# A larger padding tile on the right side of SBUF: 96 bytes become 1504

## The chip, the core and the metric

The kernel runs on one core of one Trainium2 chip. The metric is the device time of one launch in microseconds; lower is better. Times of a kernel are given as the median of several runs, and one further execution, taken by the hardware profiler, gives the trace.

## What is computed

One decoder layer on 512 tokens of width 2048, in float32:

```
h = RMSNorm(x)
[qA|kA|vA|qB|kB|vB|gA|gB] = h @ W_in                 # 2048 x 8704
yA = sliding-window attention(qA,kA,vA) @ W_branch_a  # window 128, ALiBi, sinks
yB = stick-breaking attention(qB,kB,vB) @ W_branch_b
x = x + (sigmoid(gA)*yA + sigmoid(gB)*yB) @ W_out
x = x + SwiGLU(RMSNorm(x))                            # 2048 -> 2*5632 -> 2048
out = RMSNorm_final(x)
```

## The kernel before

**Matmuls in three parts.** Each float32 operand is split into a high part (rounded to the float32r type) and a low remainder. A product is three float32r matmuls: high by high, high by low, low by high. ScalarE writes the high part of a weight chunk (`whi`, line 153) and VectorE the low part (`wlo`, line 154), from a raw chunk that SyncE's queue has loaded. A matmul has a stationary operand of 128 columns (512 bytes in each partition), loaded into the array ahead of it, and a moving operand that streams through, mostly 512 columns (2048 bytes in each partition).

**Stages, in order.**
1. Input projection. `features` (lines 340 to 342) has weights stationary and the activations `fh`, `fl` moving, 512 columns wide: 896 chunks of three matmuls, and 96 matmuls of the same shape at lines 451 to 453. `tokens` (lines 356 to 358) has `fh`, `fl` stationary and weights moving, 256 columns wide: 960 matmuls. The two attentions run in small pieces between these.
2. Branch projections: `features` again, the same lines 340 to 342, now with `yh`, `yl` moving: 768 matmuls.
3. Output projection: `rows` (lines 856 to 858), `mh`, `ml` stationary, weights moving: 768 matmuls.
4. Feed-forward: `product` (lines 256 to 258), forms `fx` stationary, weights moving. It uses a Strassen-like scheme with seven products named p1 to p7. The gate-and-up part takes 11 groups x 7 names x 4 chunks x 12 matmuls = 3696; a chunk j reads the form pairs 2j and 2j+1, six matmuls each. The down projection takes 1848, again twelve to a chunk, six for each of two pairs. At its start the forms come back from DRAM through GpSimd's queue (`load_forms`, line 1022).

**Where the tiles lie.** SBUF is filled from both ends. From the left: pool `cp` (constants), pool `wp` (raw, whi, wlo: three buffers of 4096 bytes each) and pool `tp` (47 slots of 2048 bytes: `yh`, `yl`, attention tiles, and much else). From the right: pool `pad` with one tile, then `ep` (32 slots of 2048 bytes: `fh`, `fl`, and later `mh`, `ml`), then `ca` (attention constants, 10240 bytes). After the output projection `ep` and `ca` are closed and pool `fp` takes their place below `pad` (21 form slots of 2048 bytes, and eight raw chunks).

The built program gives these addresses (bytes within a partition): `wp` starts at 18944 (whi at 31232, wlo at 43520) and `tp` at 55808, all of them 512 modulo 2048; `tp` ends at 152064. On the right, `pad` lies at 229248, the first slot of `ep` at 227200 and the lowest tile of `ca` at 153472; the slots of `ep` and `fp` are at 1920 modulo 2048. Between the two sides 1408 bytes are free.

**Forms on both sides.** In the gate-and-up part, the form pairs 0 to 4 lie in `tp`, the pairs 5 to 7 in `fp` (`form_slot`, line 866):

```
if p >= 5:
    return fp.tile([P, T], F32R, tag="fx", name=uid("fx"), bufs=21)
return slot("fx", F32R)
```

So of a name's four chunks, j = 0 and j = 1 read left-hand forms only, j = 2 one left and one right, j = 3 right-hand forms only. In the down projection, of every two forms one is in `fp` and one in `tp` (`load_forms`).

**Order of work.** Each engine follows the order of the program; the tile framework puts in the waits between a tile's writer, its readers and the next writer of the same buffer. The weights are filled two chunks ahead (`Weights.fill`), and the buffers of a chunk come free when its matmuls have run. The padding tile is read by nothing; GpSimd clears it at the start (line 114).

Of the kernel before, what the change touches and what calls it, by code (L numbers as in the profile page):

```python
# [9 lines left out]
F32 = mybir.dt.float32  # L10
# [6 lines left out]
P = 128  # L17
# [28 lines left out]
def kernel(  # L46
# [15 lines left out]
    nc = tc.nc  # L62
# [6 lines left out]
    tp = ctx.enter_context(tc.tile_pool(name="tp", bufs=47))  # L69
    early = ctx.enter_context(ExitStack())  # L70
    pad = ctx.enter_context(tc.tile_pool(name="pad", bufs=1, side="right"))
    unused = pad.tile([P, 24], F32, tag="pad", name="pad")
    ep = early.enter_context(tc.tile_pool(name="ep", bufs=32, side="right"))
    ca = early.enter_context(tc.tile_pool(name="ca", bufs=1, side="right"))
    ps = ctx.enter_context(tc.tile_pool(name="ps", bufs=4, space=bass.MemoryType.PSUM))
# [21 lines left out]
    def const(s, w, dt=F32):  # L97
        return cp.tile([P, w], dt, tag=s, name=s)
# [12 lines left out]

    ident = const("ident", P)
    make_identity(nc, ident)
    nc.gpsimd.memset(unused, 0.0)
    ones = const("ones", P)
    nc.vector.memset(ones, 1.0)

# [776 lines left out]
    for n in range(4):  # L894
        tag = ("mm", "at")[n % 2]
# [225 lines left out]
```

## Time and profile before

| | us |
|---|---|
| median of 3 runs | 2548.81 (2547.82 to 2552.52) |
| the profiled execution | 2547.38 |
| its span, first to last instruction | 2545.4 |
| TensorE busy in the span | 2502.8 |
| VectorE busy | 1980.7 |
| ScalarE busy | 1377.4 |
| GpSimd busy | 251.4 |

Busy time is how long an engine had an instruction running; overlapping matmuls are counted once. The mean duration of one matmul in the profile is longer than the distance between the starts of two neighbours, because a matmul is still draining when the next has begun. The distance of starts is what a stream of matmuls costs.

### The profile page before, as it was taken

How to read it: one execution, taken by the hardware profiler on the slowest of the kernel's cores; microseconds unless marked ns; L12 is line 12 of the kernel's file. 1: busy time of each engine (PE TensorE's matmuls, PEld its weight loads, DVE VectorE, ACT ScalarE, POOL GpSimd, SP SyncE). 2: the span in 40 equal slices, each digit the busy share in tenths (PEclk: the TensorE clock that was granted, in tenths of full speed). 3: DMA queues.
4: the chain of work that ended last, by engine and by line, in shares of the span. 5: the costliest groups of instructions: out<-in, count | busy, mean ns of one | idle time of the engine just before them, and what ended most of it. 6: DMA issues, size and time to landing. Idle time of an engine off the chain costs nothing.

```text
span 2545.4 us, 33168 instructions
## 1 busy us (share of the span) xinstructions
PE 2502.8 (98%) x11529; PEld 2065.6 (81%) x11529; DVE 1980.7 (78%) x3457; ACT 1377.4 (54%) x2626; POOL 251.4 (10%) x482
## 2 busy tenths in 40 slices
PE   9999999999999999999999999999999999999997
PEld 8888878888887788888788888888888877888886
DVE  5688888888769644375788788888888877888888
ACT  6567777667657533265554555544555544333335
POOL 0000001111101000000010011100111024302100
PEclk9999999999999999999999999999999999999999
DMA  5232333333323644344456655566555689958652
GB/s 174 91 100 92 100 108 100 96 96 104 109 89 97 201 147 149 128 162 133 148 168 193 181 180 180 171 186 183 182 173 182 188 259 324 351 159 272 183 184 88
DMA packets 256295, 407.99 MB, mean 160 GB/s; under 512 B 16480, under 2 KB 103552, under 8 KB 256128
## 3 DMA queue, kind: packets, MB, share of 16 engines
q1 hardware_dynamic: 202096, 304.13, 38.5%
q0 software_dynamic: 46912, 89.15, 11.3%
q10 hardware_dynamic: 7120, 12.61, 1.3%
q8 instruction: 90, 1.47, 0.2%
q14 instruction: 77, 0.63, 0.1%
HBM read 344.48 MB, written 61.34 MB: 159 GB/s over the span
## 4 chain that ended last, share of the span: by engine, by line
PE 63%; issue 2%; ACT 1%; POOL 0%; DVE 0%; DMA 0%; ACTq 0%; POOLq 0%; DVEq 0%
PE mm L256 9%; PE mm L258 9%; PE mm L257 9%; PE at L256 7%; PE at L258 7%; PE at L257 7%; PE mm L341 3%; PE mm L342 3%; PE mm L340 3%; PE mm L856 1%; PE mm L857 1%; PE mm L858 1%; PE at L856 1%; PE at L858 1%; PE at L857 1%
## 5 line engine op out<-in xcount | busy, mean ns | idle before, releaser
L153 ACT CAST whi<-wx 128x1024 fp32r<-128x1024 f32 x264 | 277.2, 1050 | 333.5 <-PE at L258 150.5
L257 PE MATMUL mm<-wlo,fx 128*128 128x512 f32 x1056 | 417.3, 395 | 0.5 <-DVE wlo L154 0.5
L258 PE MATMUL mm<-whi,fx 128*128 128x512 f32 x1056 | 415.5, 393 | 0.0
L154 DVE TENSOR_TENSOR wlo<-wx,whi 128x1024 fp32r<-128x1024 f32 x264 | 322.6, 1223 | 112.4 <-ACT whi L153 110.5
L154 DVE TENSOR_TENSOR wlo<-raw,whi 128x1024 fp32r<-128x1024 f32 (+1 forms) x201 | 244.1, 1215 | 185.9 <-ACT whi L153 184.5
L256 PE MATMUL mm<-whi,fx 128*128 128x512 f32 x1056 | 375.7, 396 | 10.6 <-DMA fx<-f1p 5.5
L153 ACT CAST whi<-wz 128x1024 fp32r<-128x1024 f32 x198 | 207.8, 1050 | 283.0 <-PE mm L258 144.4
L342 PE MATMUL mm<-fh,wlo 128*128 128x512 f32 x896 | 354.9, 396 | 1.5 <-DVE wlo L154 1.5
L340 PE MATMUL mm<-fh,whi 128*128 128x512 f32 x896 | 354.8, 396 | 0.0
L341 PE MATMUL mm<-fl,whi 128*128 128x512 f32 x896 | 354.5, 396 | 0.0
L153 ACT CAST whi<-raw 128x1024 fp32r<-128x1024 f32 (+1 forms) x201 | 209.7, 1044 | 220.0 <-PE mm L341 131.2
L258 PE MATMUL at<-whi,fx 128*128 128x512 f32 x792 | 311.3, 393 | 0.0
L257 PE MATMUL at<-wlo,fx 128*128 128x512 f32 x792 | 310.8, 392 | 0.0
L593 ACT COPY turned<-z 32x128 f32<-32x128 f32 (+3 forms) x888 | 242.5, 273 | 106.0 <-DVE z L753 58.0
L154 DVE TENSOR_TENSOR wlo<-wz,whi 128x1024 fp32r<-128x1024 f32 x198 | 240.2, 1221 | 53.8 <-ACT whi L153 53.6
L256 PE MATMUL at<-whi,fx 128*128 128x512 f32 x792 | 279.8, 394 | 0.7 <-ACT whi L153 0.7
L256 PEld LDWEIGHTS mm<-whi,fx 128*128 128x128 f32 x1056 | 199.1, 189 | 53.9 <-DMA fx<-f1p 5.7
L257 PEld LDWEIGHTS mm<-wlo,fx 128*128 128x128 f32 x1056 | 199.5, 189 | 45.2 <-DVE wlo L154 1.7
L258 PEld LDWEIGHTS mm<-whi,fx 128*128 128x128 f32 x1056 | 199.5, 189 | 43.1
L342 PEld LDWEIGHTS mm<-fh,wlo 128*128 128x128 f32 x896 | 169.3, 189 | 42.2 <-DVE wlo L154 2.8
L341 PEld LDWEIGHTS mm<-fl,whi 128*128 128x128 f32 x896 | 169.5, 189 | 37.5
L340 PEld LDWEIGHTS mm<-fh,whi 128*128 128x128 f32 x896 | 169.2, 189 | 36.5
(254 smaller groups left out, 4177.8 us busy)
## 6 DMA issues: line engine op xcount, KB each, us to landing
raw<-in_w_in_dram SPq DMA_DIRECT2D x135, 512.0 KB, 3.6
raw<-in_w_ffn_in_dram SPq DMA_DIRECT2D x88, 512.0 KB, 3.7
wz<-in_w_ffn_in_dram SPq DMA_DIRECT2D x88, 512.0 KB, 4.4
wx<-in_w_ffn_in_dram SPq DMA_DIRECT2D x44, 512.0 KB, 4.4
raw<-in_w_ffn_down_dram SPq DMA_DIRECT2D x44, 512.0 KB, 4.2
wz<-in_w_ffn_down_dram SPq DMA_DIRECT2D x44, 512.0 KB, 5.0
raw<-in_w_out_dram SPq DMA_DIRECT2D x32, 512.0 KB, 3.6
wx<-in_w_ffn_down_dram SPq DMA_DIRECT2D x22, 512.0 KB, 5.5
```

The costliest lines, as they stand in the source:

```text
L153: nc.scalar.copy(hi[:, :n], raw[:, :n])
L154: nc.vector.tensor_tensor(out=lo[:, :n], in0=raw[:, :n], in1=f(hi[:, :n]), op=ALU.subtract)
L256: mm(banks[t], lhsT=hi, rhs=wh[:, kk, :], start=one, stop=False, skip_group_check=True)
L257: mm(banks[t], lhsT=hi, rhs=wl[:, kk, :], start=False, stop=False, skip_group_check=True)
L258: mm(banks[t], lhsT=lo, rhs=wh[:, kk, :], start=False, stop=end, skip_group_check=True)
L340: mm(b, lhsT=wh[:, kk, c], rhs=hi[k], start=(k == 0), stop=False)
L341: mm(b, lhsT=wh[:, kk, c], rhs=lo[k], start=False, stop=False)
L342: mm(b, lhsT=wl[:, kk, c], rhs=hi[k], start=False, stop=(k == nk - 1))
L593: copy(t4[c * Q : (c + 1) * Q, :, r], z4[r * Q : (r + 1) * Q, :, c])
L856: mm(banks[t], lhsT=hi[k][:, c], rhs=wh[:, kk, :], start=(k == 0), stop=False)
L857: mm(banks[t], lhsT=hi[k][:, c], rhs=wl[:, kk, :], start=False, stop=False)
L858: mm(banks[t], lhsT=lo[k][:, c], rhs=wh[:, kk, :], start=False, stop=(k == nk - 1))
```

## The change

The padding tile grows from 24 to 376 float32 columns, 96 to 1504 bytes in each partition. Everything to the right of the free gap, that is all slots of `ep`, `ca` and `fp`, moves down by 1408 bytes. No buffer is added or taken, and no other instruction changes, save that GpSimd clears 8 columns of the padding tile in place of all 24.

```diff
-    unused = pad.tile([P, 24], F32, tag="pad", name="pad")
+    unused = pad.tile([P, 376], F32, tag="pad", name="pad")
...
-    nc.gpsimd.memset(unused, 0.0)
+    nc.gpsimd.memset(unused[:, :8], 0.0)
```

## Rows read from the trace of the kernel before

**Rows 1.** The page: span and busy time by engine, granted TensorE clock in 40 slices.
```profile
span 2545.4 us, 33168 instructions
...
PE 2502.8 (98%) x11529; PEld 2065.6 (81%) x11529; DVE 1980.7 (78%) x3457; ACT 1377.4 (54%) x2626; POOL 251.4 (10%) x482
...
PEclk9999999999999999999999999999999999999999
```
**Rows 2.** Waits of TensorE, longest first: us in total, times, longest.
```profile
PE mm L256 <- DMA fx<-f1p: 5.5, 1, 5.5
PE mm L256 <- ACT whi L153: 5.1, 1, 5.1
PE at L417 <- DMA grow<-in_norm_ffn_g_dram: 4.3, 1, 4.3
```
**Rows 3.** Matmul groups by shape: count, busy us, mean ns of one, idle before.
```profile
L342 PE MATMUL mm<-fh,wlo 128*128 128x512 f32 x896 | 354.9, 396 | 1.5 <-DVE wlo L154 1.5
...
L342 PE MATMUL mm<-yh,wlo 128*128 128x512 f32 x256 | 99.6, 389 | 0.0
...
L356 PE MATMUL mm<-whi,fh 128*128 128x256 f32 x320 | 90.0, 282 | 0.0
...
L615 PE MATMUL at<-kah,q 128*128 128x256 f32 x64 | 16.1, 281 | 0.0
```
**Rows 4.** Three stretches with one kind of matmul each: us, TensorE busy and count, clock.
```profile
62.60:84.60 22.00, 22.00 (x97) 17.83 (x96) 6.85 (x9) 5.41 (x7) 0.00 (x0) 1.00 0.31 95
870.00:1036.00 166.00, 166.00 (x735) 137.47 (x734) 76.40 (x117) 60.22 (x77) 0.00 (x0) 1.00 0.46 149
1040.00:1212.00 172.00, 172.00 (x742) 139.46 (x741) 96.82 (x260) 86.61 (x198) 6.64 (x12) 1.00 0.43 138
```
**Rows 5.** TensorE in order of time, one name of the gate-and-up part.
```profile
1610.14 0.62 PE L256 MATMUL mm<-whi,fx 128*128 128x512 f32 x2
...
1612.87 0.62 PE L256 MATMUL mm<-whi,fx 128*128 128x512 f32 x2
...
1615.59 0.62 PE L256 MATMUL mm<-whi,fx 128*128 128x512 f32 x2
...
1618.35 0.63 PE L256 MATMUL mm<-whi,fx 128*128 128x512 f32 x2
```
**Rows 6.** The same view, a chunk j = 3 that nothing interrupts.
```profile
1642.23 0.64 PE L256 MATMUL at<-whi,fx 128*128 128x512 f32 x2
...
1644.09 0.40 PE L258 MATMUL at<-whi,fx 128*128 128x512 f32 x1
1644.33 0.40 PE L256 MATMUL at<-whi,fx 128*128 128x512 f32 x1
1644.57 0.39 PE L257 MATMUL at<-wlo,fx 128*128 128x512 f32 x1
...
1645.03 0.39 PE L256 MATMUL mm<-whi,fx 128*128 128x512 f32 x1
```
**Rows 7.** The same view, four attention matmuls among the input projection.
```profile
164.49 0.39 PE L658 MATMUL at<-ph,vv 128*128 128x512 f32 x1
...
165.43 0.39 PE L340 MATMUL mm<-fh,whi 128*128 128x512 f32 x1
```
**Rows 8.** The chain of waits at the start of the down projection.
```profile
2046.63 0.53 POOL f19p L990
...
2097.45 0.54 POOL x L1008
2098.00 5.72 DMA fx<-f1p
```
**Rows 9.** Stretches of gate-and-up and down: columns as in rows 4 (PE, PEld, DVE).
```profile
1500.00:1800.00 300.00, 300.00 (x1341) 245.72 (x1340) 251.03 (x286) 155.44 (x209) 25.86 (x49) 1.00 0.60 180
...
2300.00:2530.00 230.00, 230.00 (x999) 187.67 (x998) 197.20 (x215) 95.29 (x112) 24.73 (x46) 1.00 0.56 176
```
**Rows 10.** GpSimd in order of time, the clearing of the padding tile.
```profile
0.95 0.12 POOL L114 MEMSET pad<- 128x24 f32 x1
```
**Rows 11.** Instructions on the tiles `yh`: durations ns min/median/max, first and last start us.
```profile
L340 PE MATMUL mm<-yh,whi x256: 387/389/399, 863.9 to 1037.3; 128*128 128x512 f32 x128
```

## The prediction

> **What bounds the kernel now.** I read the page first: TensorE is busy for 2502.8 of 2545.4 us, VectorE for 78% and ScalarE for 54%, and the granted clock stands at 9 tenths or more of its higher level, 2.4 GHz, in every slice [rows 1]. Then I read what TensorE waited for: the three longest waits are 5.5, 5.1 and 4.3 us, once each [rows 2]. All its idle time is 2545.4 - 2502.8 = 42.6 us. So the kernel is a nearly unbroken stream of matmuls, and the only quantity that can move it much is the distance between the starts of two of them. The question for a change of addresses is whether this distance depends on where the operands lie.
>
> The trace answers it, because this kernel runs the same lines with operands on either side. I took stretches that hold one kind of 512-column matmul and divided the time by the count (one or two of the count still run from before the stretch, so I take off two) [rows 4]:
> - `features` with `fh`, `fl` moving, on the right: 22.00 / 95 = 231.6 ns.
> - `features` with `yh`, `yl` moving, on the left, the same three lines: 166.00 / 733 = 226.5 ns.
> - `rows` with `mh`, `ml` stationary, on the right: 172.00 / 740 = 232.4 ns.
>
> All three at a granted clock of 1.00, with no idle TensorE. The mean durations of single matmuls say the same: 396 ns with `fh`, 389 ns with `yh` on line 342 [rows 3]. These are different stages, though, so I looked for both sides within one stage. In the gate-and-up part, chunks j = 0 and j = 1 have their forms on the left, j = 2 half and half, j = 3 on the right. At 1610.14 us a name begins: its chunks of twelve take 2.73, 2.72 and 2.76 us [rows 5]; the fourth holds transposes, so for j = 3 I take an undisturbed one, 1642.23 to 1645.03, 2.80 us [rows 6]. That is 227, 227, 230 and 233 ns for a matmul, with the same neighbours on VectorE and ScalarE within 35 us. The weights lie on the left throughout. So a matmul whose two operands both lie on the left, at the same offset modulo 2048 in steps of 512, costs 227 ns, and one with an operand on each side costs 5 to 6 ns more, whichever operand it is.
>
> **The change, part by part.** The right side moves down by 1408 bytes: 1920 - 1408 = 512, the offset of the left side. If the extra 5 to 6 ns hang on the offset, all right-hand matmuls come to the left-hand spacing. The terms:
>
> 1. *Input projection, `fh` and `fl` moving.* 3 x 896 + 96 = 2784 matmuls. Per matmul, at least 231.6 - 226.5 = 5.1 ns [rows 4], at most 396 - 389 = 7 ns [rows 3]. I take 5.7, between them, near the difference that the longer stretch of `rows` shows (232.4 - 226.5 = 5.9): 15.9 us, bounds 14.2 and 19.5.
> 2. *Output projection, `mh` and `ml` stationary.* 768 matmuls at 232.4 - 226.5 = 5.9 ns, or 5.4 if they only come to the 227 of the left-hand chunks [rows 4, 5]: I take 5.6, 4.3 us, bounds 4.1 and 4.5.
> 3. *Feed-forward, right-hand forms.* In gate-and-up 3 of 8 pairs, 3696 x 3/8 = 1386; in down one of two, 924; together 2310. Per matmul (2.80 - 2.72) / 12 = 6.7 ns by the undisturbed chunks; by the mixed chunk (2.76 - 2.72) / 6 = 6.7 ns too, the starts being read to 0.01 us, so each is good to about 1 ns [rows 5, 6]. I take 6: 13.9 us, bounds 11.5 (5 ns) and 15.4.
> 4. *256-column matmuls of `tokens`, `fh` and `fl` stationary, 960.* The nearest all-left rows of that width are the attention scores: 281 ns against 282 [rows 3]. I take nothing. Bounds: the difference of the wide ones, 5.7 x 960 = 5.5 us gained, and, since 281 against 282 leaves 1 ns either way, 1 us lost.
> 5. *The clearing.* 0.12 us on GpSimd at 0.95 us after the start [rows 10], off TensorE's path; less of it changes nothing that I can see.
> 6. *The order and the waits.* No tile gains or loses a buffer. `pad`, `ep`, `ca` and `fp` move together, so each slot of `fp` covers the same slots of `ep` and `ca` as before, and waits for the same readers. The 1408 bytes are just those that were free. VectorE's and ScalarE's pieces are the same; where an address changes their speed, they have room: VectorE is busy 251.03 of 300 us in gate-and-up and 197.20 of 230 in down [rows 9], 84 and 86%, which a stream of matmuls 1.5% denser makes 85 to 87%.
>
> Against this stands what the stream gives back. Where TensorE waits for a chain that other engines set, it comes to the wait earlier by what it saved while the chain ran. The longest such chain is GpSimd's queue from 2046.63 to 2098.00, which issues the loads of the forms, ending in the wait for `f1p` [rows 8]: 51 us, some 220 matmuls, half of them on the right, 6 ns each: 0.7 us. The others are shorter; I take 1.2 us for all.
>
> Sum: 15.9 + 4.3 + 13.9 - 1.2 = 32.9 us. The profiled execution took 2547.38, the median of the runs is 1.43 above it; 2548.81 - 32.9 = 2515.9. I say 2516, which is 1.3% less.
>
> By the bounds: at most 19.5 + 4.5 + 15.4 + 5.5 = 44.9, that is 2504; at least 14.2 + 4.1 + 11.5 - 1 - 3 (more given back) = 25.8, that is 2523.
>
> **A rule that speaks against it.** The rows show a distance of starts that goes with the side on which an operand lies: 226.5 and 231.6 ns on the same three lines [rows 4]. The Trainium skill, page "SBUF — State Buffer", section "Who interferes with whom", gives TensorE two independent read ports, one for the moving operand and one for the weights, and says that "PE and ACT never wait on anyone". By that rule the place of an operand costs nothing and the change is worth nothing: 2548.8. The trace does not agree with it as far as it goes; that is rival A.
>
> **The rivals.**
>
> *A. Nothing moves.* The extra 5 to 6 ns belong to the right-hand part of the memory itself, or to something that goes with those tiles, and not to the offset; then 2548.8, within 5 us. For it: the trace holds right-hand tiles at one offset only, so side and offset can't be told apart in it. Also for it: four attention matmuls with both operands in `tp` go from 164.49 to 165.43, 235 ns each, though all of it lies on the left [rows 7]; so the common offset alone doesn't assure 227. Against it: these are a few dozen, between right-hand neighbours, while whole stages and thousands of forms on the left keep 227 from addresses 31232 up to 152064, so far apart that a border just above would be a strange chance.
>
> *B. The common offset is the bad one for right-hand tiles: slower.* Some right-hand matmuls are 0.24 us apart already, as from 1644.09 to 1644.33 and to 1644.57 [rows 6]. If a right-hand tile at 512 met the weights in this way every time, the 2784 + 768 + 2310 = 5862 matmuls would cost 240 - 232.4 = 7.6 ns more: 45 us, 2593. It turns to slower by over 5 us as soon as their mean spacing rises by 0.9 ns. Against it: left-hand tiles at that very offset, with the same weights, show none of it over 166 us [rows 4].
>
> *C. The stream speeds up, but the feed of the down projection doesn't follow.* There GpSimd's queue loads the forms as buffers come free and VectorE is at 86% [rows 9], and the wait of 5.5 us at the start shows that the loads can be late [rows 2, 8]. If each later part waited for its loads, the 924 x 6 = 5.5 us of the down projection would go, and with a like sum at its start some 10 us in all: 2526. Against it: from 2300 to 2530 TensorE has no idle time at all [rows 9].
>
> **How the numbers follow.** The forecast as it stands gets 0.84, A 0.07, B 0.04, C 0.05. A measurement of this kernel tells about 0.2%, 5 us, from no change. The forecast and C are faster: 0.89; A is the same: 0.07; B is slower: 0.04. The forecast's own range is 2504 to 2523; with C it reaches 2528, and the range 2504 to 2528 leaves out A, B and a little at each edge.
>
> **What would show it.** In the profile after: line 342 with `fh` at a mean of 389 ns in place of 396; lines 856 to 858 at 389 as well; all four chunks of a gate-and-up name at 2.72 us unless a transpose lies in them; the span shorter by about 16 us when the branch projections begin (863.9 us before [rows 11]), by 20 when the feed-forward does, and by 33 at the end; the branch projections unchanged. The steps fail if `fh` falls and `mh` or the right-hand forms don't (then moving and stationary operands differ), or if none falls (A). The prediction is wrong if the spacing stays at 232, or if it comes to 227 and new idle time before TensorE takes up more than 10 us.

## The result, and the profile after

The changed kernel takes 2522.24 us, median of 4 runs (2522.17 to 2522.51), against 2548.32 for the kernel before on the same chip: 0.9895 of its time, 95% interval 0.9878 to 0.9912. That is 26.1 us less; 32.9 were forecast, and the time lies within the range of 2504 to 2528, less than 1 us inside the forecast's own edge of 2523. The profiled execution took 2522.17 us, and every engine runs the same instructions in the same order as before, but for the clearing of the padding tile.

The page: TensorE's busy time has fallen by 30.5 us, its idle time (span less busy time) has risen from 42.6 to 47.9 [rows 1].

```profile
span 2520.2 us, 33168 instructions
...
PE 2472.3 (98%) x11529; PEld 2063.9 (82%) x11529; DVE 1979.0 (79%) x3457; ACT 1378.9 (55%) x2626; POOL 251.4 (10%) x482
```

Matmul groups by shape (columns as in [rows 3]). `fh` moving has come from 396 to 391 ns, `mh` stationary stands at 389, like the all-left `yh`, which hasn't moved. The 256-column `tokens` have gone up by 1 ns.

```profile
L342 PE MATMUL mm<-fh,wlo 128*128 128x512 f32 x896 | 350.8, 391 | 4.0 <-DVE wlo L154 3.9
...
L342 PE MATMUL mm<-yh,wlo 128*128 128x512 f32 x256 | 99.6, 389 | 0.0
...
L356 PE MATMUL mm<-whi,fh 128*128 128x256 f32 x320 | 90.3, 283 | 0.0
...
L857 PE MATMUL mm<-wlo,mh 128*128 128x512 f32 x128 | 49.8, 389 | 0.0
```

Two stretches of one kind each (columns as in [rows 4]), `yh` above, `mh` below. With two of each count taken off, both are 160.00 / 705 = 227.0 ns; `mh` was at 232.4. For `fh` and `fl` the mean of all distances of starts in the trace (those above 300 ns, where something interrupts, left out, as in all such means below) falls from 232.6 to 227.5.

```profile
870.00:1030.00 160.00, 160.00 (x707) 132.50 (x706) 73.86 (x114) 58.55 (x74) 0.00 (x0) 1.00 0.44 144
1040.00:1200.00 160.00, 160.00 (x707) 132.50 (x706) 93.59 (x252) 84.73 (x195) 6.63 (x12) 1.00 0.43 140
```

The starts of five chunks of twelve in the gate-and-up part, from TensorE in order of time: at 1592.21 a chunk j = 3 (all right), then j = 0 and 1 (all left) and j = 2 (mixed). All four take 2.72 us; they took 2.80, 2.73, 2.72 and 2.76 [rows 5, 6].

```profile
1592.21 0.61 PE L256 MATMUL at<-whi,fx 128*128 128x512 f32 x2
...
1594.93 0.61 PE L256 MATMUL mm<-whi,fx 128*128 128x512 f32 x2
...
1597.65 0.61 PE L256 MATMUL mm<-whi,fx 128*128 128x512 f32 x2
...
1600.37 0.61 PE L256 MATMUL mm<-whi,fx 128*128 128x512 f32 x2
...
1603.09 0.62 PE L256 MATMUL mm<-whi,fx 128*128 128x512 f32 x2
```

The same view, the four attention matmuls of [rows 7], whose tiles all lie on the left and have not moved: 0.91 us where they took 0.94.

```profile
162.16 0.39 PE L658 MATMUL at<-ph,vv 128*128 128x512 f32 x1
...
163.07 0.39 PE L340 MATMUL mm<-fh,whi 128*128 128x512 f32 x1
```

When the branch projections begin, only 7.0 us have been gained (856.9 for 863.9 [rows 11]), where 16 were forecast:

```profile
L340 PE MATMUL mm<-yh,whi x256: 389/389/389, 856.9 to 1030.3; 128*128 128x512 f32 x128
```

What TensorE waited for (us, times, longest). The first three are nearly as before [rows 2]; `wlo` at line 342 is new in this size, 3.9 in place of 1.5 [rows 3].

```profile
PE mm L256 <- DMA fx<-f1p: 5.8, 1, 5.8
PE mm L256 <- ACT whi L153: 5.1, 1, 5.1
PE at L417 <- DMA grow<-in_norm_ffn_g_dram: 4.3, 1, 4.3
PE at L658 <- ACT ph L598: 4.2, 1, 4.2
PE mm L342 <- DVE wlo L154: 3.9, 4, 1.8
```

One such wait costs twice. The end of the windowed attention, first in the kernel before, then in the changed one (columns as in [rows 4]): TensorE's idle time is 3.45 and then 4.37 us, and the granted clock, which falls from 2.4 to 1.2 GHz after the wait, stays low for longer, with a mean of 0.94 and then 0.89 of the higher level over these 30 us.

```profile
340.00:370.00 30.00, 26.55 (x109) 21.15 (x108) 21.73 (x51) 24.26 (x58) 0.00 (x0) 0.94 0.24 74
```

```profile
340.00:370.00 30.00, 25.63 (x101) 20.37 (x100) 22.58 (x49) 23.94 (x53) 0.00 (x0) 0.89 0.23 71
```

The start of the feed-forward shows the same in its clock alone, again before and then after. The wait there is 5.1 us in both kernels, but the granted clock of the 22 us around it is 0.84 and then 0.77. Why it stays low for longer there isn't shown.

```profile
1210.00:1232.00 22.00, 16.39 (x67) 12.75 (x66) 14.93 (x34) 13.80 (x29) 2.16 (x4) 0.84 0.67 239
```

```profile
1200.00:1222.00 22.00, 16.35 (x66) 12.74 (x66) 16.34 (x36) 14.10 (x30) 2.16 (x4) 0.77 0.67 239
```

### The profile page after: what moved, and what is told of

Read it like the earlier page. It is cut to its first block, busy times and chain, and to the rows that moved or that the text cites. A ratio compares the mean times of both kernels' runs of the same rounds, so it can differ in the third digit from the quotient of the medians.

```text
span 2520.2 us, 33168 instructions
## 1 busy us (share of the span) xinstructions
PE 2472.3 (98%) x11529; PEld 2063.9 (82%) x11529; DVE 1979.0 (79%) x3457; ACT 1378.9 (55%) x2626; POOL 251.4 (10%) x482
## 4 chain that ended last, share of the span: by engine, by line
PE 62%; issue 2%; DVE 1%; ACT 1%; POOL 0%; DMA 0%; ACTq 0%; POOLq 0%; DVEq 0%
PE mm L257 9%; PE mm L258 9%; PE mm L256 9%; PE at L256 7%; PE at L257 7%; PE at L258 7%; PE mm L340 3%; PE mm L341 3%; PE mm L342 3%; PE at L858 1%; PE mm L856 1%; PE mm L858 1%; PE at L856 1%; PE at L857 1%; PE mm L857 1%
## 5 line engine op out<-in xcount | busy, mean ns | idle before, releaser
L258 PE MATMUL at<-whi,fx 128*128 128x512 f32 x792 | 308.4, 389 | 0.0
L256 PE MATMUL at<-whi,fx 128*128 128x512 f32 x792 | 276.3, 389 | 0.7 <-ACT whi L153 0.7
```

The source lines that it names most:

```text
L256: mm(banks[t], lhsT=hi, rhs=wh[:, kk, :], start=one, stop=False, skip_group_check=True)
L258: mm(banks[t], lhsT=lo, rhs=wh[:, kk, :], start=False, stop=end, skip_group_check=True)
```

## The experiments

Three questions were open: do the stages add up as the steps say; which distance between the sides counts; and where some 7 us went. Each ratio is to runs of the kernel before that were made beside the run in question (medians from 2548.3 to 2549.1 us).

**One part of the change alone.** e1 puts the larger padding under the feed-forward's pool only, e2 under the input projection's pools only.

```diff
 # e1: padding tile of 24 columns, and before pool fp is opened:
+pad2 = ctx.enter_context(tc.tile_pool(name="pad2", bufs=1, side="right", ...))
+unused2 = pad2.tile([P, 352], F32, tag="pad2", name="pad2")
 # e2: the same tile in a pool that closes with ep and ca
+pad2 = early.enter_context(tc.tile_pool(name="pad2", bufs=1, side="right"))
```

> Only pool fp (feed-forward forms and chunks) moves to offset 512; ep and ca stay at 1920. Theory (each matmul pays for its own two operands): fh and mh keep 231 to 233 ns, all fx come to 227; 2310 x 6 = 13.9 us less, 1 to 2 given back: 2535 to 2537. Rival (the gain of the change comes from the input projection alone and the feed-forward is held by its feed): under 5 us less, 2543 or more.

> Only ep and ca (fh, fl, mh, ml, attention constants) move to 512; fp stays at 1920. Theory: fh and mh at 227 ns, right-hand fx at 233; 14 + 4 us less from the spacing, and most of what the change gave back to waits appears here, in the attention stage: 5 to 7 us; so 2535 to 2538. Rival (what was given back lies in the feed-forward): 2530 to 2531.

e1 took 2532.96 us, 0.9939 of before (0.9922 to 0.9956), 16.1 us less; e2 2537.18, 0.9954 (0.9939 to 0.9969), 11.9 less. Together 28.0, the whole change 26.1: the parts add up to within 2 us, and in the spans of the traces more closely (14.4 + 10.5 = 24.9 against 25.2). e1 lies 2 to 4 us below its forecast, e2 within its own. The windows show that each stage follows the place of its own right-hand tiles. e1, `mh` at the old place (160.00 / 688 = 232.6 ns), then the down projection (200.00 / 882 = 226.8):

```profile
1040.00:1200.00 160.00, 160.00 (x690) 129.73 (x689) 95.88 (x259) 85.83 (x197) 6.64 (x12) 1.00 0.44 142
2300.00:2500.00 200.00, 200.00 (x884) 165.68 (x883) 172.88 (x179) 81.42 (x89) 20.41 (x38) 1.00 0.59 187
```

e2, the same two stretches: the other way round (227.0, and 200.00 / 867 = 230.7).

```profile
1040.00:1200.00 160.00, 160.00 (x707) 132.55 (x706) 93.59 (x252) 84.72 (x195) 6.64 (x12) 1.00 0.44 140
2300.00:2500.00 200.00, 200.00 (x869) 163.20 (x869) 169.82 (x175) 79.87 (x88) 20.54 (x39) 1.00 0.59 187
```

e2 also begins the branch projections at 856.9 us, like the full change, so the 7.0 us belong to its first stage alone.

Within a stage, neighbours pay too. In the down projection of the kernel before, six matmuls with right-hand forms alternate with six with left-hand ones. The last left-hand one of six is 232.0 ns from the next start and the first 231.0, the four between them 226.8 to 227.3 (means of 149 each, the last part, which goes by threes, left out); in the changed kernel all six lie between 226.4 and 227.0.

**Which distance counts.** Four other paddings; e4 moves the left side too. The numbers at the right are the places modulo 2048.

```diff
-    unused = pad.tile([P, 376], F32, tag="pad", name="pad")
+    unused = pad.tile([P, 120], F32, tag="pad", name="pad")   # e3: right side at 1536
+    unused = pad.tile([P, 280], F32, tag="pad", name="pad")   # e4: right side at 896,
+    lunused = lpad.tile([P, 96], F32, tag="lpad", name="lpad")  #     and left at 896
+    unused = pad.tile([P, 312], F32, tag="pad", name="pad")   # e5: right side at 768
+    unused = pad.tile([P, 360], F32, tag="pad", name="pad")   # e11: right side at 576
```

> Padding of 480 bytes: right-hand tiles at 1536 modulo 2048, left at 512; equal modulo 512 and 1024, not modulo 2048. If equality modulo 2048 is what counts: spacing 231 to 233 ns with one operand on each side, 2545 to 2550. If modulo 512 is enough (the weights' slices lie at all four multiples of 512 and cost 227 in all): 227 ns, 2520 to 2524.

> A padding of 384 bytes on the left too, and 1120 on the right: all tiles at 896 modulo 2048, equal to each other, none at a multiple of 512. If the distance between the two operands counts: 227 ns everywhere, 2520 to 2524. If each operand's own place counts (a multiple of 512): every matmul at 231 to 233, the left-hand ones too: 2565 to 2580.

> Padding of 1248 bytes: right-hand tiles at 768 modulo 2048, 256 away from the left side modulo 512. Equality modulo 512 is what counts: 231 to 233 ns with one operand on each side, 2545 to 2550. Equality modulo 256 is enough: 227 ns, 2520 to 2524.

> Padding of 1440 bytes: right-hand tiles at 576 modulo 2048, 64 away from the left side modulo 256. If only a distance of 128 modulo 256 is bad: 227 ns, 2520 to 2524. If the distance has to be 0 modulo 256, or modulo 128: 231 to 240 ns with one operand on each side, 2545 or more.

| run | right less left, mod 2048 | us | of before (95%) |
|---|---|---|---|
| changed kernel | 0 | 2522.24 | 0.9895 (0.9878 to 0.9912) |
| e4, both at 896 | 0 | 2523.15 | 0.9898 (0.9883 to 0.9913) |
| e3 | 1024 | 2521.84 | 0.9895 (0.988 to 0.991) |
| e5 | 256 | 2522.58 | 0.9899 (0.9883 to 0.9916) |
| e11 | 64 | 2549.40 | 1.0006 (0.9997 to 1.0015) |
| before | 1408 = 5 x 256 + 128 | 2548.32 | |

The same stretch of `mh` in e3, e4, e5 and e11, one after the other:

```profile
1040.00:1200.00 160.00, 160.00 (x707) 132.49 (x706) 93.81 (x252) 84.73 (x195) 6.64 (x12) 1.00 0.43 140
```

```profile
1040.00:1200.00 160.00, 160.00 (x708) 132.48 (x707) 93.69 (x252) 84.75 (x195) 6.64 (x12) 1.00 0.43 140
```

```profile
1040.00:1200.00 160.00, 160.00 (x708) 132.48 (x707) 94.10 (x252) 85.48 (x196) 6.67 (x12) 1.00 0.44 143
```

```profile
1040.00:1200.00 160.00, 160.00 (x687) 128.93 (x686) 94.14 (x252) 85.93 (x196) 6.65 (x12) 1.00 0.43 140
```

About 707 matmuls in 160 us at a distance of 0, 256 or 1024, and 687 (160.00 / 685 = 233.6 ns) at 64. So it is the distance between the two sides that counts, not the place of either (e4), and equality modulo 2048 is more than is needed: the three distances tried that are multiples of 256 are all good. The fallen theories are the first one of e3 (modulo 2048), the second of e4 (each operand's own place), the first of e5 (modulo 512), and the first of e11 (that only 128 is bad).

These paddings move the right-hand tiles for every engine alike, so they don't say whose reads meet. A stretch in which VectorE, ScalarE and GpSimd do nothing does: the end of the output projection, first in the kernel before, then in the changed one (columns TensorE, weight loads, VectorE, ScalarE, GpSimd).

```profile
1202.30:1214.30 12.00, 12.00 (x53) 9.72 (x52) 0.00 (x0) 0.00 (x0) 0.00 (x0) 1.00 0.27 87
```

```profile
1191.25:1203.15 11.90, 11.90 (x54) 9.87 (x53) 0.00 (x0) 0.00 (x0) 0.00 (x0) 1.00 0.27 88
```

By the starts, 52 distances of `mh` from 1202.33 to 1214.42 have a mean of 232.5 ns, and 51 from 1191.43 to 1202.99 one of 226.7: the difference is whole without the other engines. Nor are transfers needed: 30 matmuls of `mh` in the kernel before and 33 in the changed one have no DMA packet and no other engine at work from 0.3 us before their start to the end of the next, and they lie at 232.4 and 226.7 ns. What is left of what the change moved is the two operands that TensorE reads itself.

**Where the rest went: load or chains.** e6 moves two of every 16 transposing copies from VectorE to ScalarE in both attentions, e8 does so in the kernel before; e7 and e12 set the windowed attention's pieces out more thinly or more densely (`pace` is how many of them come due at each step of the matmul stream).

```diff
-            split_turned(z, NT, ph, pl, 10)          # e6, e8
+            split_turned(z, NT, ph, pl, 12)
-            split_turned(z, NT - j, oh, ol, 8)
+            split_turned(z, NT - j, oh, ol, 10)
...
-        pace[0] = 0.36
+        pace[0] = 0.33                               # e7; 0.39 in e12
```

> The changed kernel with two more of every 16 transposing copies on ScalarE in both attentions (12 and 10 in place of 10 and 8). Theory (the 8 us given back are waits in the attention stages for a VectorE that is 88% busy there and that the denser stream outruns): the waits between 320 and 362 us and near 800 us fall from some 15 us to under 9, 2514 to 2518. Rival (the waits are the length of single chains, not VectorE's load): ScalarE's copies are slower, 273 ns against 217, the chains get longer, 2522 to 2526.

> The kernel before with the same shift of copies to ScalarE. Spacing stays at 232. Theory: before, the stream was slower and VectorE just kept up, so the shift is worth less here than in the changed kernel: 1 to 3 us, 2545 to 2547. Rival: it is worth as much or as little in both, because the waits have nothing to do with the density of the stream.

> The changed kernel with the windowed attention's pieces set out more thinly (pace 0.33 in place of 0.36). If VectorE's load in that stage is what TensorE waits for, pieces spread over more matmuls take 2 to 5 us of waits away: 2517 to 2520; the pieces moved behind the stage may bring them back later: 2522. Rival (single chains): no change, 2521 to 2523.

> The changed kernel with the windowed attention's pieces set out more densely (pace 0.39 in place of 0.36), since thinner cost 3 us. If the waits at the end of that stage come from pieces left over there: 2517 to 2520. If VectorE then falls behind earlier in the stage: 2523 to 2528.

e6 took 2529.59 us (0.9928 of before, 0.9913 to 0.9943), 7 more than the changed kernel and more than either theory said. e8 took 2557.17 (1.0034, 1.0021 to 1.0047), 9 more than before. So the loss is about the same with the old spacing as with the new, as the rival of e8 has it, and taking load from VectorE at ScalarE's cost doesn't shorten the waits: those for ScalarE's results at the end of the attention chains grew, in e6 from 4.2 to 7.4 us at line 658, and new ones at line 729:

```profile
PE at L658 <- ACT ph L598: 7.4, 5, 3.4
...
PE at L729 <- ACT a L743: 3.8, 3, 2.0
```

e7 took 2525.56 (0.9912, 0.9897 to 0.9926), 3 more, against both its theories; e12 2522.24 (0.9897, 0.9882 to 0.9912), no gain and between its two forecasts. These four also change the order in which pieces and matmuls are issued, so none of them singles out one cause. No version of the whole computation beats the changed kernel by more than the runs differ.

**Where the rest went: the chains taken away.** e9 (the changed kernel) and e10 (the kernel before) replace the 16 copies by one, which leaves the blocks in the wrong places. The two have the same order of instructions, save the clearing.

```diff
-        t = unblock(z, n, share)[:, : n * P]
+        t = slot("turned")[:, : n * P]
+        nc.scalar.copy(t, z[:, : n * P])
```

> The changed kernel with the 16 small copies after each block transpose in both attentions replaced by one ScalarE copy of the whole tile (the blocks then stay in the wrong places: part of the computation is left out). VectorE and ScalarE have far less to do there. Theory (the 8 us given back are waits for the attentions' chains, which a denser stream reaches earlier): the waits at 323, 334, 349 to 362, 778 and 798 us, 13.4 us together with the slow clock after them, go: 2503 to 2511, and 31 to 34 us less than the kernel before with the same cut. Rival (the shortfall lies in the spacing or elsewhere): 26 us less than that kernel, as now.

> The kernel before with the same cut (the blocks stay in the wrong places). Spacing of the right-hand matmuls stays at 231 to 233 ns; its attention waits at 355 and 805 us, 7.4 us, go: 2536 to 2543. Theory: 31 to 34 us above the changed kernel with the cut. Rival: 26 above.

e9 took 2498.31 us, e10 2531.41: 33.1 apart, as the theory said, though both fell by more than forecast (24 and 17 us less than with the copies; 11 to 19 and 5 to 12 were expected). The page, e9 and then e10:

```profile
span 2495.8 us, 31687 instructions
...
PE 2462.9 (99%) x11529; PEld 2061.5 (83%) x11529; DVE 1845.8 (74%) x2777; ACT 1214.1 (49%) x1926; POOL 250.1 (10%) x482
```

```profile
span 2530.0 us, 31687 instructions
...
PE 2497.2 (99%) x11529; PEld 2063.2 (82%) x11529; DVE 1848.3 (73%) x2777; ACT 1212.0 (48%) x1926; POOL 249.8 (10%) x482
```

TensorE's idle time is 32.9 and 32.8 us: where the attentions' chains don't hold it, both kernels wait alike, and the whole difference, 2497.2 - 2462.9 = 34.3 us, is spacing. Added up from start to start by kind of matmul in the two traces, it is 14.3 us for `fh` and `fl` with 512 columns, 4.4 for `mh` and `ml`, 16.1 for the feed-forward, -0.9 for `tokens`, and 0.4 for all else.

## Why the prediction was right, and which term was wrong

**The mechanism was right; its size was right in total, and there luck had a part.** Terms 1 to 3 came to 34.1 us before anything was given back, and the pair e9 and e10 measures 34.3. But two terms were off by some 2 us each, in opposite ways. Term 1, 15.9 us: the pair gives 14.3, at the lower bound; `fh` came from 395 to 390 ns in the mean there, and from 396 to 391 with the change, where 389 were forecast. Term 2, 4.3 us: 4.4. Term 3, 13.9 us: 16.1, above its upper bound of 15.4. By the mean distances in the two traces the right-hand forms gave some 12.8 us (from 232.6 to 232.9 ns down to 226.7 to 227.8), a little less than forecast, and the left-hand ones, which the steps put at nothing, some 3.8: they stood next to right-hand ones. That neighbours matter was in [rows 7]: those four attention matmuls came from 0.94 to 0.91 us with their own tiles where they were. Term 4, nothing: 0.9 us lost, near the bound given.

**The term that was mis-sized is what the stream gives back: 1.2 us forecast, about 9 measured** (34.3 less the 25.2 by which the span fell). The step looked for the longest chain in the list of waits and found GpSimd's at the start of the down projection; that wait grew by 0.3 us only, from 5.5 to 5.8. (Of the 220 matmuls it counted there, three in eight read right-hand forms, not half; that makes 0.2 us.) Some 7 us went in the first stage: it gained 7.0 us where term 1 alone measures 14.3, and e2, with the feed-forward at the old place, starts the branch projections at the same 856.9. About 2 us went in the feed-forward, which took 14.2 us less from start to start where the pair shows 16.1. TensorE's idle time grew by 5.3 us in the whole span; what remains, 34.3 - 30.5 = 3.8 us, is busy time, and most of it is the lower granted clock: 0.05 of 30 us at the end of the windowed attention and 0.07 of 22 us at the start of the feed-forward, 1.5 us of full clock each. That the waits in the first stage hang on the attentions' chains is shown by e9 and e10, where they are gone and the difference is whole. Which engine's part of a chain is the tight one is not settled: relieving VectorE made it worse.

**The rivals.** A fell: the spacing moved with the address, and its evidence, the attention matmuls, moved with it. So the rule of the Trainium skill behind it ("SBUF — State Buffer", "Who interferes with whom", that PE never waits on anyone and that its two read ports are independent) doesn't cover this case: the same 768 matmuls of `mh` take 227.0 or 232.4 ns, with only an address changed. The trace doesn't show TensorE waiting for another engine, for the difference is whole with the others idle; it is the independence of its own two reads that the runs don't bear out. How the two get in each other's way isn't shown. B fell: of the right-hand matmuls only the 256-column ones are slower, by 1 ns. C, a feed of the down projection that doesn't follow, fell too; what was given back went for the most part in the attention stages, and the wait it started from grew by 0.3 us.

## What to carry to other kernels

Where TensorE is busy without a break, compare the spacing of equal matmuls whose operands lie in different pools; if it differs, bring the pools to a distance of a multiple of 256 bytes (0, 256 and 1024 modulo 2048 were tried here), which one padding tile can do. Compare within a stage, and count the matmuls next to the badly placed ones as well. And when a stream gets denser, price what it gives back at each stage where another engine's chain already ends in a wait, the clock after the wait included, rather than at the longest wait alone.

## What was not expected of the hardware

A distance of 64 bytes between the operands costs `mh` 6.6 ns a matmul (233.6 for 227.0), no less than the 1408 of the kernel before does (5.4); distances of 256 and 1024 cost nothing. Shorter steps than 64 were not tried. Other than that, the change left VectorE's and ScalarE's instruction times nearly alone: VectorE's busy time went from 1980.7 to 1979.0 us, ScalarE's from 1377.4 to 1378.9.
